# A bilinear form on one core: the first weights as two 64-partition halves, and smaller pieces at the end

**Chip, cores, metric.** One core of a Trainium2 chip. The metric is device time in microseconds (us), of the whole execution; the span that the profile shows is about 1.75 us shorter. In the profiles PE is TensorE, PEld its weight loads, DVE VectorE, ACT ScalarE, POOL GpSimd and SP SyncE; "clock" is the share of TensorE's full clock that was granted.

## The reference

```python
batch, dim_i, dim_j, dim_k = 32, 256, 256, 128        # all float32
np.einsum('bi,bj,kij->bk', x, y, weight)
```

The weights are 128 x 256 x 256 float32, 33.6 MB; x and y are 32 KB each.

## The kernel before

The outputs are done in 32 groups of 4 values of k. A group's weights are a tile of 128 partitions (32 pieces of i times 4 of k) by 8 x 256. Group 0 comes as float32 through SyncE's queue and is cast by ScalarE; groups 1 to 31 come through GpSimd's queue, cast to bfloat16 by the DMA, each into a buffer of its own.

```python
x_sb = consts.tile([B, I], f32);  nc.scalar.dma_start(out=x_sb, in_=x)
y_sb = consts.tile([B, J], f32);  nc.scalar.dma_start(out=y_sb, in_=y)
w0 = consts.tile([P, IC * J], f32)
nc.sync.dma_start(out=w0, in_=w_v[0])
def split(g):
    return [(0, 4), (4, 6), (6, 8)] if g == G - 1 else [(0, IC)]
# load(g): one GpSimd DMA for each piece of split(g), into its own bf16 tile
... # x_rep, transposes, mask products -> xblk; y -> y4; w0 cast to w0b
for g in range(G):
    ps = pso.tile([P, J], f32)
    for ic in range(IC):
        nc.tensor.matmul(out=ps, lhsT=xblk[:, ic], rhs=w_tiles[g, ic], ...)   # cut
    nc.vector.tensor_tensor_reduce(out=tmp, in0=ps, in1=y4, ..., accum_out=acc[:, g:g+1])
nc.sync.dma_start(out=out_v, in_=acc)
```

## Time and profile before

| | before |
|---|---|
| time, median | 88.63 us at first (3 runs), 88.59 beside the change (4 runs) |
| span of the profile (of a run of 88.90 us) | 87.1 us |
| busy: PE, DVE, POOL | 62%, 21%, 21% |
| DMA strip at 90% or more | 37 of 40 slices |
| last weights landed / PE done | 83.40 / 84.30 us |

The prediction below shows the lines that carry this. Two views are added here for comparison with those after. The first is the table of stretches for the head (columns: stretch, its length, busy time and count of PE, PEld, DVE, ACT and POOL, granted clock, DMA share, GB/s written):

```profile
3.00:4.00 1.00, 0.96 (x8) 0.94 (x8) 1.00 (x7) 0.00 (x0) 1.00 (x3) 1.00 0.89 318
4.00:5.00 1.00, 0.11 (x1) 0.00 (x0) 0.89 (x3) 0.00 (x0) 1.00 (x3) 1.00 0.92 353
5.00:6.00 1.00, 0.42 (x2) 0.28 (x2) 1.00 (x3) 0.00 (x0) 1.00 (x3) 1.00 1.15 320
```

While w0 flows as float32, 318 to 353 GB/s are written. The second is the page's list of DMA issues (KB each, us from issue to landing):

```profile
w<-in_weight_dram SPq DMA_DIRECT2D x1, 1024.0 KB, 5.3
...
x_sb<-in_x_dram ACTq DMA_DIRECT2D x1, 32.0 KB, 1.7
y_sb<-in_y_dram ACTq DMA_DIRECT2D x1, 32.0 KB, 4.0
```

x is there 1.7 us after its issue, w0 after 5.3.

### The profile page before, as it was taken

Reading aid. Unit: us, or ns where it says so; the run is one execution under the profiler, and the core shown is the slowest. Engines: PE = TensorE matmul, PEld = TensorE weight load, DVE = VectorE, ACT = ScalarE, POOL = GpSimd, SP = SyncE. Lnnn points to the kernel's source line nnn. Section 1 sums busy time; section 2 is a strip of 40 time slices with the busy share of each in tenths; the row PEclk is TensorE's granted clock in tenths of the full one; section 3 lists DMA queues with packets and bytes.
Section 4 is the critical chain, followed back from the end, with each engine's and each line's share of the span. In section 5 each row is a group of like instructions: output and inputs, shape, how many; then the busy total and the mean of one; then the engine's idle time right before and its main releaser. Section 6 shows DMA issues by size and latency. Waiting matters only on the chain.

```text
span 87.1 us, 741 instructions
## 1 busy us (share of the span) xinstructions
PE 54.4 (62%) x268; PEld 32.6 (37%) x268; DVE 18.6 (21%) x79; ACT 3.3 (4%) x3; POOL 18.3 (21%) x39
## 2 busy tenths in 40 slices
PE   0416994667777843776487773754887544974870
PEld 0415653433343432433344432332444331543630
DVE  0893123011111120111101111111011211031030
ACT  2327000000000000000000000000000000000000
POOL 5980222222111221112222222012222200000000
PEclk9999999755555696557955598589555975569659
DMA  1899999999999999999999999999999999999700
GB/s 30 277 312 209 216 216 216 213 213 213 213 214 213 211 213 218 213 216 213 213 213 213 211 216 213 211 213 216 213 218 211 213 214 211 214 214 203 127 3 8
DMA packets 5139, 17.43 MB, mean 200 GB/s; under 512 B 720, under 2 KB 1040, under 8 KB 5008
## 3 DMA queue, kind: packets, MB, share of 16 engines
q0 software_dynamic: 4752, 16.26, 93.6%
q1 hardware_dynamic: 288, 1.07, 3.5%
q10 hardware_dynamic: 96, 0.07, 0.4%
q8 instruction: 2, 0.03, 0.1%
q14 instruction: 1, 0.01, 0.0%
HBM read 33.62 MB, written 0.02 MB: 386 GB/s over the span
## 4 chain that ended last, share of the span: by engine, by line
DMA 87%; PE 4%; POOL 3%; issue 2%; DVE 0%; POOLq 0%; DVEq 0%
DMA w<-in_weight_dram 87%; PE ps L137 4%; POOL w L60 3%; DVE tmp L144 0%; POOL ident L68 0%; POOL ident L67 0%; POOLq L68 0%; POOLq L165 0%; DVEq L176 0%
## 5 line engine op out<-in xcount | busy, mean ns | idle before, releaser
L137 PE MATMUL ps<-w,xblk 128*128 128x256 bf16 x248 | 50.8, 377 | 24.2 <-DMA w<-in_weight_dram 24.2
L137 PEld LDWEIGHTS <-xblk 128*128 128x128 bf16 x256 | 31.0, 130 | 46.9 <-DMA w<-in_weight_dram 34.3
L60 POOL DMA_DIRECT2D w<-in_weight_dram x33 | 17.7, 546 | 50.6 <-DMA w<-in_weight_dram 49.8
L144 DVE CUSTOM_DVE_ANT_0 tmp<-ps,y 128x256 f32<-128x256 f32 x32 | 13.6, 425 | 62.2 <-PE ps L137 62.2
L137 PE MATMUL ps<-w0b,xblk 128*128 128x256 bf16 x8 | 2.1, 411 | 1.6 <-ACT w0b L129 1.6
L91 PE MATMUL xt_ps<-ident,x_rep 32*128 32x32 f32 x8 | 1.1, 293 | 3.0 <-POOL ident L68 3.0
L144 DVE DVE_READ_ACCUMULATOR2_ANT acc<- 128x1 f32 x32 | 2.7, 83 | 0.0
L100 DVE TENSOR_SCALAR xblk<-xt_ps,mask 128x256 bf16<-128x256 f32 x4 | 2.5, 771 | 0.1
L129 ACT CAST w0b<-w 128x1024 bf16<-128x1024 f32 x2 | 2.0, 1042 | 3.2 <-DMA w<-in_weight_dram 3.2
L91 PEld LDWEIGHTS xt_ps<-ident,x_rep 32*128 32x128 f32 x8 | 0.9, 200 | 3.0 <-POOL ident L68 3.0
L85 DVE COPY x_rep<-x_sb 32x128 f32<-32x128 f32 x8 | 1.3, 236 | 2.4 <-DMA x_sb<-in_x_dram 2.4
L129 ACT ACT_TABLE_LOAD x1 | 1.3, 1283 | 1.6 <-PEq L165 1.6
L109 PE MATMUL yt_ps<-ident,y_sb 32*128 32x32 f32 x2 | 0.4, 300 | 1.1 <-DMA y_sb<-in_y_dram 1.1
L109 PEld LDWEIGHTS yt_ps<-ident,y_sb 32*128 32x128 f32 x2 | 0.3, 199 | 1.2 <-DMA y_sb<-in_y_dram 1.2
L125 DVE COPY y<-y_ps 128x256 f32<-128x256 f32 x1 | 0.4, 425 | 1.3 <-PE y_ps L119 1.3
L119 PE MATMUL y_ps<-ident,yt 128*128 128x128 f32 x2 | 0.6, 417 | 0.0
L119 PEld LDWEIGHTS y_ps<-ident,yt 128*128 128x128 f32 x2 | 0.4, 226 | 0.1
L114 DVE COPY yt<-yt_ps 128x256 f32<-128x256 f32 x1 | 0.4, 448 | 0.0
L76 DVE TENSOR_REDUCE mask<-ident 128x4 f32<-128x128 f32 x1 | 0.4, 369 | 0.0
L68 POOL TENSOR_SCALAR_AFFINE_SELECT ident<-ident 128x128 f32<-128x128 f32 x1 | 0.3, 322 | 0.1
L67 POOL MEMSET ident<- 128x128 f32 x1 | 0.2, 224 | 0.0
L165 POOL MEMSET const-float32-0.0<- 128x1 f32 x1 | 0.1, 99 | 0.2 <-issue 0.2
(3 smaller groups left out, 0.3 us busy)
## 6 DMA issues: line engine op xcount, KB each, us to landing
w<-in_weight_dram POOLq DMA_DIRECT2D x30, 512.0 KB, 19.4
w<-in_weight_dram SPq DMA_DIRECT2D x1, 1024.0 KB, 5.3
w<-in_weight_dram POOLq DMA_DIRECT2D x1, 256.0 KB, 18.3
w<-in_weight_dram POOLq DMA_DIRECT2D x2, 128.0 KB, 15.6
x_sb<-in_x_dram ACTq DMA_DIRECT2D x1, 32.0 KB, 1.7
y_sb<-in_y_dram ACTq DMA_DIRECT2D x1, 32.0 KB, 4.0
out_dram<-acc SPq DMA_DIRECT2D x1, 16.0 KB, 1.4
```

The costliest lines, as they stand in the source:

```text
L60: nc.gpsimd.dma_start(out=wt, in_=w_v[g][:, :, lo * J:hi * J])
L76: nc.vector.tensor_reduce(out=mask, in_=ident.rearrange("p (ip kk) -> p kk ip", kk=KK), axis=mybir.AxisListType.X, op=add,)
L85: nc.vector.tensor_copy(out=x_rep[:, ic, :, :], in_=x_cols[:, ic, :].unsqueeze(2).to_broadcast([B, IP, KK]),)
L91: nc.tensor.transpose(out=xt_ps[:, ic, :], in_=x_rep[:, ic, :, :].rearrange("b ip kk -> b (ip kk)"), identity=ident[:B, :B],)
L100: nc.vector.tensor_scalar(out=xblk[:, :, :, kk], in0=xt_ps, scalar1=mask[:, kk:kk + 1], scalar2=None, op0=mult,)
L109: nc.tensor.transpose(out=yt_ps[:, jh, :], in_=y_sb[:, jh * P:(jh + 1) * P], identity=ident[:B, :B],)
L114: nc.vector.tensor_copy(out=yt4, in_=yt_ps.unsqueeze(3).to_broadcast([P, JH, B, KK]))
L119: nc.tensor.transpose(out=y4_ps[:, jh * P:(jh + 1) * P], in_=yt4[:, jh, :, :].rearrange("p b kk -> p (b kk)"), identity=ident,)
L125: nc.vector.tensor_copy(out=y4, in_=y4_ps)
L129: nc.scalar.copy(out=w0b[:, lo * J:hi * J], in_=w0[:, lo * J:hi * J])
L137: nc.tensor.matmul(out=ps, lhsT=xblk[:, ic, :, :].rearrange("p b kk -> p (b kk)"), rhs=w_tiles[g, ic], start=(ic == 0), stop=(ic == IC - 1),)
L144: nc.vector.tensor_tensor_reduce(out=tmp, in0=ps, in1=y4, scale=1.0, scalar=0.0, op0=mult, op1=add, accum_out=acc[:, g:g + 1],)
```

## The change

The intent: get the first weights under way sooner by issuing them from two queues at once and letting x and y wait; and shorten the work that is left when the last weights have landed.

```diff
-    x_sb = consts.tile([B, I], f32)
-    nc.scalar.dma_start(out=x_sb, in_=x)
-    y_sb = consts.tile([B, J], f32)
-    nc.scalar.dma_start(out=y_sb, in_=y)
     w0 = consts.tile([P, IC * J], f32)
-    nc.sync.dma_start(out=w0, in_=w_v[0])
+    PH = P // 2
+    with tc.manual_schedule(engines={mybir.EngineType.SP, mybir.EngineType.Activation}):
+        for h, eng in enumerate((nc.sync, nc.scalar)):
+            eng.dma_start(out=w0[h * PH:(h + 1) * PH, :],
+                          in_=w_v[0][h * PH // KK:(h + 1) * PH // KK])
+        x_sb = consts.tile([B, I], f32)
+        nc.scalar.dma_start(out=x_sb, in_=x)
+        y_sb = consts.tile([B, J], f32)
+        nc.sync.dma_start(out=y_sb, in_=y)
     def split(g):
-        return [(0, 4), (4, 6), (6, 8)] if g == G - 1 else [(0, IC)]
+        if g == G - 1:
+            return [(0, 4), (4, 6), (6, 7), (7, 8)]
+        if g == G - 2:
+            return [(0, 4), (4, 8)]
+        return [(0, IC)]
```

Below, "head" is the part down to y, "tail" is the new split.

More of the change, by code (lines that the diff above doesn't have):

```diff
@@ L41 @@
     w_v = weight.rearrange("(kk g) (ip ic) j -> g ip kk (ic j)", kk=KK, ic=IC)
-    x_sb = consts.tile([B, I], f32)
-    nc.scalar.dma_start(out=x_sb, in_=x)
-    y_sb = consts.tile([B, J], f32)
-    nc.scalar.dma_start(out=y_sb, in_=y)
     w0 = consts.tile([P, IC * J], f32)
-    nc.sync.dma_start(out=w0, in_=w_v[0])
-    def split(g):
-        return [(0, 4), (4, 6), (6, 8)] if g == G - 1 else [(0, IC)]
+    PH = P // 2
+    with tc.manual_schedule(engines={mybir.EngineType.SP, mybir.EngineType.Activation}):
+        for h, eng in enumerate((nc.sync, nc.scalar)):
+            eng.dma_start(
+                out=w0[h * PH:(h + 1) * PH, :],
+                in_=w_v[0][h * PH // KK:(h + 1) * PH // KK],
+            )
+        x_sb = consts.tile([B, I], f32)
+        nc.scalar.dma_start(out=x_sb, in_=x)
+        y_sb = consts.tile([B, J], f32)
+        nc.sync.dma_start(out=y_sb, in_=y)
+    def split(g):
+        if g == G - 1:
[3 more added lines that the diff above has]
+        return [(0, IC)]
     w_tiles = {}
```

## The prediction

> **What bounds the kernel now.** I read the page first: the busy rows, the strip of 40 slices, the chain that ended last.
>
> ```profile
> PE 54.4 (62%) x268; PEld 32.6 (37%) x268; DVE 18.6 (21%) x79; ACT 3.3 (4%) x3; POOL 18.3 (21%) x39
> ...
> DMA  1899999999999999999999999999999999999700
> ...
> DMA 87%; PE 4%; POOL 3%; issue 2%; DVE 0%; POOLq 0%; DVEq 0%
> ```
>
> No compute engine is full, while the DMA engines are at 90% or more in 37 of the 40 slices (2.2 us each). 87% of the chain is one thing, weights arriving. HBM read is 33.62 MB; one group is 1 MiB of float32, written as 0.5 MiB of bfloat16. In the trace's record of single packets, one engine starts a 4096-byte packet every 305 ns and a new group every 2.457 us: 8 packets are 2.440, so a group boundary costs 17 ns. 1.049 MB in 2.457 us is 427 GB/s read. This middle, about 31 x 2.457 = 76 us, is the floor; the change doesn't touch it. Only the head (before the stream flows) and the tail (after it stops) can move. For the head I read the order in time:
>
> ```profile
> 0.74 0.37 ACTq L44 DMA_DIRECT2D x_sb<-in_x_dram  x1
> 0.74 0.62 SPq L50 DMA_DIRECT2D w<-in_weight_dram  x1
> 1.14 0.45 ACTq L46 DMA_DIRECT2D y_sb<-in_y_dram  x1
> 1.24 0.66 POOL L60 DMA_DIRECT2D w<-in_weight_dram  x1 [0.80 <-POOLq L165]
> ...
> 2.42 1.33 DVE L85 COPY x_rep<-x_sb 32x128 f32<-32x128 f32 x8 [2.42 <-DMA x_sb<-in_x_dram]
> ...
> 6.09 1.99 ACT L129 CAST w0b<-w 128x1024 bf16<-128x1024 f32 x2 [3.19 <-DMA w<-in_weight_dram]
> ...
> 7.19 0.58 PE L137 MATMUL ps<-w0b,xblk 128*128 128x256 bf16 x2 [1.58 <-ACT w0b L129]
> ```
>
> Issues start at 0.74. By the packet records x moves from 1.75, w0 from 2.15; w0's packets last till 5.1 to 5.75, engine by engine, and on each engine the first packet of POOL's queue starts 6 ns after w0's last. So POOL's stream of groups 1 to 31 is ready and waits for w0: whatever w0 gains or loses moves the whole stream. For the tail, the chain in order of time:
>
> ```profile
> 61.29 19.52 DMA w<-in_weight_dram
> 80.81 0.05 issue
> 80.85 3.44 PE ps L137 x16
> 84.30 0.02 issue
> 84.32 0.42 DVE tmp L144
> ```
>
> The last 3.44 us are not a transfer. Group 30 lands whole at 80.81; then 16 matmuls run without a gap. By the semaphore records the pieces of group 31 land at 82.06, 82.76 and 83.40, while PE begins their matmuls at about 82.57, 83.42 and 83.85 (80.85 plus 8, 12, 14 steps of 0.214 us; 3.44 less the 0.417 duration of the last, over 15, is 0.20 to 0.21). PE is about 0.4 us behind the last landing. The granted clock there is halved:
>
> ```profile
> 81.50:82.00 0.50, 0.50 (x5) 0.36 (x3) 0.00 (x0) 0.00 (x0) 0.00 (x0) 0.50 0.86 139
> 82.00:82.50 0.50, 0.50 (x4) 0.38 (x3) 0.00 (x0) 0.00 (x0) 0.00 (x0) 0.50 0.22 35
> ```
>
> (Stretch, length, busy time of PE and PEld, then the other engines, clock, DMA share, GB/s.) PE is full at clock 0.50, while the DMA engines are already emptying. They empty unevenly: thirteen end by about 82.3, the last at 83.07. [...]
>
> [...] The trace of before[...]: w0's 1.049 MB from 2.15 to about 5.4 is some 320 GB/s. It has no 64-partition load of size, so it shows nothing on the halves. [...]
>
> **The change part by part.** (1) w0 as two 0.5 MB halves, issued at 0.74 on both queues. A transfer of 32 rows took 1.01 us from issue to first packet (0.74 to 1.75); w0, 1.41, behind x's. With a half on each queue and nothing ahead I put the first weight packet at 1.75 to 1.9: 0.25 to 0.4 us earlier. (2) x now moves inside the stream instead of in front of it: 32 packets of 45 ns over 16 engines plus two 9 ns completions, 0.1 us back. Head gain before contention: 0.15 to 0.3, say 0.25. (3) Contention on partitions: [...] My estimate is a median loss of 0.2, with a long tail.
>
> (4) x and y come later, behind halves: y took 4.0 us to land before, and now x will too, about 4.8 to 5.4 instead of 2.39. Behind it lie the copies (1.33), the transposes (about 0.3 more), four mask products (4 x 0.771, 2.5 with overlap): xblk at about 9.5 instead of 6.63, the first main matmul there instead of 7.19. That is 2.3 us late on PE, but not in the end: a group needs 8 x 0.214 = 1.7 us of PE against 2.457 us of arrival, so PE regains 0.7 per group and is level after four groups or so. Each group's weights have a buffer of their own, so POOL's issues wait for landings, never for PE.
>
> (5) Group 30 in two, group 31 ending in two single steps: two more issues on POOL at 0.53 us, done near 70 us, off the path. In the stream: two boundaries of 17 ns, plus the smaller packets. A 1024-byte packet costs 78.6 ns a start against 305 / 4 = 76.3, so about 3 ns is fixed per packet; 8 more packets of 2048 instead of 4096 cost 24 ns, 8 more of 512 another 24. In all 0.08 us later for the last landing, 83.48.
>
> (6) The tail with it: the first half of group 30 lands 1.23 us before the second, at 79.6, when PE is idle (group 29 ends at 79.5), so its four matmuls move into the gap. The second half at 80.85 ends by 81.5. Then PE waits for the first piece of 31, at 82.1: four to 82.98, two to 83.41, one to 83.62, and the last starts at 83.62, its weights there since 83.48, and ends 0.42 later, 84.04. Before: 84.28. Gain 0.24. The last split itself gives perhaps 0.05 of that; the split of group 30 does the rest.
>
> Sum: -0.25 head, +0.2 contention, -0.24 tail: -0.29 us. From 88.63: about 88.35, which I put as 88.4.
>
> **Rivals.** A: [...] w0 lands [...] later and drags the stream[...]. For it: [...] that POOL's stream waits for w0. Against: w0's first packets took 714 ns where later ones took 309[...]. Partly true is likely, wholly 1 in 8. B: the late x becomes the bound, PE never catches up. For: PE 62% busy at a mean clock of 0.73. Against: 24.2 us of idle time of PE behind weights, ten times the delay. It would cost at most 2.3 us if no slack were there; I give it under 3%. C: everything works, the halves overlap each other's start latency (0.4 us from 714 against 309), and the stragglers are milder: 0.4 more, 87.8. D: the tail isn't PE's but the last engine's: then the split gives nothing and costs 0.08; total near 88.6.
>
> **Range and chances.** Every part is small against 1.77 us, which 2% is. Upward only rival A reaches 89.5 or more[...]. Downward, head and tail at their best give 0.4 + 0.4, 87.8. So 87.8 to 89.5, with 4% for slower and 2% for faster.
>
> **What would show it.** The first weight packets near 1.8 instead of 2.15, and POOL's first group landing up to 0.3 earlier than 8.60: step 1; if it lands later, contention (step 3) is larger. The first CAST from w0 would move from 6.09 likewise. The first main matmul near 9.5 with PE level with the landings by group 6: step 4. In the chain, the run of 16 matmuls at the end replaced by one of about 8, behind a landing near 82: step 6. A final stretch where each matmul waits for its own landing would mean that DMA, not PE, sets the end. The middle, 2.457 us a group, must not change. Wrong would be: w0 landing after 7 us, a gap in the DMA strip between w0 and group 1, or PE still behind at 70 us.

The sum came to -0.29 us (-0.25 + 0.2 - 0.24). Its +0.2 (step 3) was worked out from no measured number; the other two terms are reckoned from the trace of before. Of the engine that ends last the trace shows two instruction fetches of 16 KB (0.94 and 0.98 us) and one of 8 KB (0.32 us), but not on which engine. That POOL's issues wait for landings and not for PE (step 4) is in before's list of waits: 25 times, 49.8 us, for weights by DMA, and once, 0.8 us, for POOL's own sequencer at the start.

## The result, and the profile after

Ratios are the mean time of one kernel's runs over that of the other's of the same rounds, so not quite the ratio of the medians quoted. Executions over 1.5% slower than the fastest of the same kernel are left out of the means.

| | before | after |
|---|---|---|
| time, median (4 runs each) | 88.59 us (88.46 to 88.67) | 89.77 us (89.54 to 89.95) |
| ratio, 95% interval | | 1.0132 (1.0103 to 1.0162) |
| span of the profile (runs of 88.90 and 89.54 us) | 87.1 | 87.8 |
| busy: PE, POOL | 62%, 21% | 59%, 22% |

The time went up by 1.2 us. It lies outside the range that the prediction gave, 87.8 to 89.5, on the slow side. First the head, the instructions in order of time after (start us, us, engine, line, operation):

```profile
0.74 0.66 SPq L49 DMA_DIRECT2D w<-in_weight_dram  x1
0.75 0.62 ACTq L49 DMA_DIRECT2D w<-in_weight_dram  x1
...
1.40 0.60 ACTq L54 DMA_DIRECT2D x_sb<-in_x_dram  x1
1.47 0.81 SPq L56 DMA_DIRECT2D y_sb<-in_y_dram  x1
...
8.40 1.16 DVE L95 COPY x_rep<-x_sb 32x128 f32<-32x128 f32 x8 [8.40 <-DMA x_sb<-in_x_dram]
...
12.52 0.61 PE L147 MATMUL ps<-w0b,xblk 128*128 128x256 bf16 x2 [2.38 <-DVE xblk L110]
```

Both halves are issued within 10 ns of each other. But x is there only at 8.40, and PE's first main matmul begins at 12.52 where it began at 7.19. The page's DMA issues after say how long the halves took:

```profile
w<-in_weight_dram SPq DMA_DIRECT2D x1, 512.0 KB, 6.7
w<-in_weight_dram ACTq DMA_DIRECT2D x1, 512.0 KB, 4.4
...
x_sb<-in_x_dram ACTq DMA_DIRECT2D x1, 32.0 KB, 7.0
```

The two halves, issued together, land 4.4 and 6.7 us later: one after the other, and the second later than the whole of w0 did (5.3). The same three stretches after show the rate:

```profile
3.00:4.00 1.00, 0.00 (x0) 0.00 (x0) 0.00 (x0) 0.00 (x0) 1.00 (x3) 1.00 1.21 262
4.00:5.00 1.00, 0.00 (x0) 0.00 (x0) 0.00 (x0) 0.00 (x0) 1.00 (x3) 1.00 0.97 262
5.00:6.00 1.00, 0.00 (x0) 0.00 (x0) 0.00 (x0) 0.00 (x0) 1.00 (x3) 1.00 0.84 180
```

The engines are as busy as before, but 262 and then 180 GB/s are written instead of 320 to 353. They are not starved; each packet takes longer. The trace's record of single packets has the start, duration, size and queue of each; the engine isn't in it and has to be worked out from which packet follows on which. By it, after the change an engine does its four packets of ScalarE's half, then its four of SyncE's, and only then POOL's. Before, a settled 8192-byte packet took 309 ns; after, the settled ones take 606 ns, and 44 of the second half's 64 are over 550.

Now the tail: the chain that ended last, its end in order of time (start us, us, what), after:

```profile
75.42 9.21 DMA w<-in_weight_dram
84.63 0.04 issue
84.67 0.28 PE ps L147
84.95 0.02 issue
84.98 0.42 DVE tmp L154
```

The run of 16 matmuls is gone. One matmul stands behind the last landing, 0.32 us from landing (84.63) to the end of PE (84.95); before it was 0.90 (83.40 to 84.30). But the two ends ran at different clocks, 0.50 before and 1.00 after, so the 0.58 us between them isn't the split's alone (see the tail's runs below). The landing itself is 1.23 later, and this takes back more than the tail can have given.

### The profile page after: what moved, and what is told of

It is laid out like the page before. It is cut to its first block, busy times and chain, and to the rows that moved or that the text cites. A ratio compares the mean times of both kernels' runs of the same rounds, so it can differ in the third digit from the quotient of the medians.

```text
span 87.8 us, 746 instructions
## 1 busy us (share of the span) xinstructions
PE 51.4 (59%) x268; PEld 31.3 (36%) x268; DVE 18.5 (21%) x79; ACT 3.3 (4%) x3; POOL 19.3 (22%) x41
## 4 chain that ended last, share of the span: by engine, by line
DMA 89%; issue 5%; POOL 1%; DVE 0%; PE 0%; POOLq 0%; DVEq 0%
DMA w<-in_weight_dram 89%; POOL w L70 1%; DVE tmp L154 0%; PE ps L147 0%; POOL ident L77 0%; POOLq L186 0%; POOLq L175 0%; DVEq L186 0%
## 5 line engine op out<-in xcount | busy, mean ns | idle before, releaser
L147 PE MATMUL ps<-w,xblk 128*128 128x256 bf16 x248 | 47.9, 359 | 22.4 <-DMA w<-in_weight_dram 22.3
L147 PEld LDWEIGHTS <-xblk 128*128 128x128 bf16 x256 | 29.7, 125 | 44.2 <-DMA w<-in_weight_dram 31.9
L70 POOL DMA_DIRECT2D w<-in_weight_dram x35 | 18.7, 545 | 56.3 <-DMA w<-in_weight_dram 55.5
```

What stands on the lines that cost most here:

```text
L70: nc.gpsimd.dma_start(out=wt, in_=w_v[g][:, :, lo * J:hi * J])
L147: nc.tensor.matmul(out=ps, lhsT=xblk[:, ic, :, :].rearrange("p b kk -> p (b kk)"), rhs=w_tiles[g, ic], start=(ic == 0), stop=(ic == IC - 1),)
```

## The experiments

To compare heads without the noise of the end I use two numbers from the packet records: **w0 per engine**, the summed durations of w0's packets over 16 engines, and **sixth transfer**, the mean over engines of the time at which POOL's sixth transfer (group 6) is done on it. A mean over engines is moved little by one late engine. Times of different rows come from different chips and rounds; the ratio is to the kernel before of the same rounds. The figures that stand first in the expectations of e1, e3 to e7, e10, e11 and e14 are those of the partition theory, the prediction's rival A: a half of w0 is slow because of which 64 partitions it covers. No run shows a mechanism.

| kernel | time, median us | ratio to before | w0 per engine us | sixth transfer us | last landing us |
|---|---|---|---|---|---|
| before | 88.59 | | 2.90 | 20.31 | 83.40 |
| after | 89.77 | 1.0132 | 4.04 | 21.27 | 84.63 |
| e16, after again | 89.68 | 1.0151 | 4.47 | 21.67 | 85.00 |
| e1, head only | 89.63 | 1.0138 | 3.98 | 21.21 | 84.54 |
| e2, e12, e15, tail only | 88.11, 87.90, 88.22 | 0.9984, 0.9962, 0.9970 | 2.60, 2.70, 3.06 | 19.93, 19.84, 20.13 | 83.10, 83.00, 83.40 |
| e8, group 30 in two only | 88.07 | 0.9970 | 2.73 | 19.84 | 83.11 |
| e3, w0 whole, x and y behind | 88.54 | 1.0029 | 2.55 | 20.18 | |
| e4, halves by columns, two queues | 89.32 | 1.0124 | 3.25 | 20.80 | |
| e9, halves by columns, one queue | 89.32 | 1.0114 | 3.68 | 21.07 | |
| e5, halves by partitions, one queue | 89.15 | 1.0090 | 3.48 | 20.67 | |
| e14, middle and outer partitions | 89.48 | 1.0086 | 2.90 | 20.55 | |

### Which part costs: head or tail

e1 has the new head with the old split; e2 the old head with the new split.

> The new head (w0 as two halves of 64 partitions on two queues, then x and y) with the old tail. [...] the halves[...] cost about 1.05 us at the first group of POOL's queue (landing 8.60 before, 9.65 after) and nothing gives it back, while the old tail has 0.4 us of PE lag: 89.6 to 90.1 us, slower than the whole change; most 8192-byte packets near 606 ns. Rival (the smaller pieces at the end are what costs): near 88.6, with packets near 309 ns.

> The old head with the new tail (group 30 in two, group 31 ending in two single steps). My sum: last landing 0.08 us later, PE no longer behind it, 0.25 to 0.45 us faster than before: 88.15 to 88.4. Rival (more pieces cost more in the stream than they give): 88.6 or above.

e1: 1.0138 (1.0076 to 1.0199), e2: 0.9984 (0.9936 to 1.0032). The whole loss is the head's. e1's packets show 606 ns again. e2 gained less than the 0.25 to 0.45 us expected. Its chain ends so:

```profile
73.36 9.74 DMA w<-in_weight_dram
83.10 0.04 issue
83.14 0.28 PE ps L141
83.42 0.02 issue
```

One matmul behind the last landing, 0.32 us. The old tail, in e1, ends so:

```profile
69.95 14.58 DMA w<-in_weight_dram
84.54 0.04 issue
84.58 0.39 PE ps L142 x2
84.97 0.02 issue
```

Two matmuls and 0.43 us, not 16 and 0.90 as in the trace of before. The kept traces tell the two apart by the clock. Twelve have the old tail: in six (e1, e3, e7, e9, e11, e13) the clock is back at 1.00 before PE is done, and PE ends 0.43 to 0.44 us after the last landing; in five (before, e4, e5, e10, e14) it is 0.50 to the end, and the lag is 0.90 to 1.11; e6 lies between. At full clock the new tail's 0.32 is thus only 0.11 us better. All six traces with group 30 cut end at clock 1.00. Whether the cut brings that about or it is chance isn't shown. How much that is worth in time one run couldn't say, so it was run twice more, once beside a kernel that only cuts group 30:

```diff
+        if g == G - 2:
+            return [(0, 4), (4, 8)]
         return [(0, 4), (4, 6), (6, 8)] if g == G - 1 else [(0, IC)]
```

> The old head with the new tail once more, for the size of the tail's gain (first time 0.9984, -0.5 to +0.3%). My sum said -0.24 us; the trace of the first time has the last landing to the end of PE 0.32 us where before has 0.90, and 0.08 us more stream, so -0.2 to -0.5 us. Rival (the end is set by the slowest DMA engine, PE's lag matters not): 0 to +0.1.

> The old head and only group 30 cut in two. My step 6 has this doing most of the tail's gain: 0.05 us or so less than the whole new tail, so -0.15 to -0.45 us from before. Rival (the single steps at the end do it): no gain, 0 to +0.1.

> The old head with the new tail a third time. If step 6 is right in size: ratio 0.996 to 0.998, as the first two (0.9984, 0.9962). Rival (no gain, the two were chance): 0.999 to 1.001.

0.9962 (0.9915 to 1.0008) and 0.9970 (0.9917 to 1.0023) for the tail; 0.9970 (0.9928 to 1.0011) for the cut of group 30 alone. No single interval excludes zero. The mean of the three tail runs is 0.9972, some 0.25 us; the direction is the same in all three and in e8, and the size is near 0.24. It sits in the slower runs: of the 33 runs of the kernel before beside these three, 15 took over 88.4 us, of the tail's 18 one, while the fastest are 87.88 and 87.77. It would fit if the cut spares the runs that end at half clock, but the kept traces can't show that; e8's own trace has 0.44 us of lag at clock 1.00, no less than the old tail there. e8 gives nearly all of it beside e12 in the same rounds, as step 6 said, but the difference between the two (0.0008) is far below what these runs can tell.

### Is it the order (x and y behind the weights)?

```diff
+        nc.sync.dma_start(out=w0, in_=w_v[0])
+        nc.sync.dma_start(out=x_sb, in_=x)
+        nc.sync.dma_start(out=y_sb, in_=y)
```

> w0 in one piece of 128 partitions on SyncE, first; x and y on the same queue after it; old tail. [...] w0's packets at 309 ns, x and y late without harm, 88.5 to 88.9. Rival (the order costs: x and y land late, PE starts late): 89.3 or more. It also shows whether w0's first packet comes earlier than 2.15 when nothing is ahead of it (my step 1 said 1.75 to 1.9; the profile after says 2.15 for a half, so size and not the place behind x would set it).

1.0029 (0.9979 to 1.0078), 88.54: hardly anything, though PE's first main matmul comes at 11.12 there. Late x and y do no harm that these runs can tell. And with nothing ahead of it on any queue, w0's first packet comes at 2.42, not earlier than before (2.15); in e10 and e11, where a whole w0 is also first, it comes at 2.15. So it isn't x that holds it back.

### Is it the partitions, or having two transfers?

> The head of the change, but w0 is cut by columns and not by partitions: two transfers of 128 partitions and 4096-byte rows on the same two queues at the same time, then x and y as in the change; old tail. [...] packets near 155 ns (half of 309), first POOL group landing near 8.6 to 8.8, 88.5 to 88.9. Rival (two queues at once, whatever the cut, cost): as slow as the head alone, 89.6 or more.

The diff to the change: `w0[:, h * CH:(h + 1) * CH]` from `w_v[0][:, :, h * CH:(h + 1) * CH]` in place of the partition halves. This was a miss for the partition theory: 1.0124, 89.32 us, nearly the 89.6 that the rival wanted. The packets say something more mixed: the second half ran mostly at 159 ns per 4096 bytes (mean 167), full speed, while in the change the second half ran at 606 per 8192; but the first half averaged 240 where 155 is half of 309. Two more kernels cut w0 on SyncE's queue alone:

> The kernel with w0 whole, then x and y, all on SyncE (88.54 us), with w0 cut in two halves of 64 partitions one after the other on that same queue. [...] packets near 606 ns all through, w0's time per engine 4.0 to 4.9 us instead of 2.55, 89.7 to 90.9 us. Rival (two queues beginning at once is what costs): 88.3 to 88.9, packets near 309 ns.

> The same, with w0 cut by columns into two transfers of 128 partitions and 4096-byte rows on one queue. If it is two queues at once that made the column halves slow (89.32 us): 88.3 to 88.9 here, packets near 157 ns. If it is the 4096-byte rows: 89.1 to 89.6 again, with the early packets at 200 ns and more. [...]

e5 (partition halves, one queue): 1.0090 (1.0026 to 1.0155), less than the partition theory wanted and more than the rival did. Its trace shows another order: on one queue an engine does half 0, then about five packets of POOL's, then half 1 packet by packet between POOL's. The second half's packets average 388 ns there, against 544 in the change, where none of POOL's run between them; that this makes the difference isn't shown. Half 0, which nothing else disturbed, slows down as in the change: its last 16 packets average 597 ns. e9 (column halves, one queue): 1.0114 (1.0054 to 1.0174), slow again. So two queues are not what makes column halves slow. That left rows of 4096 bytes, or the cut as such. Two kernels for that:

```diff
+        nc.sync.dma_start(out=w0, in_=w_v[0][:, :, 0:CH])     # e13: left columns only
+    nc.gpsimd.dma_start(out=w0r, in_=w_v[0][:, :, CH:])      # right columns by POOL, bf16
```

> w0's left columns alone (128 partitions, rows of 4096 bytes, one transfer on SyncE, then x and y); the right columns come by POOL as bfloat16 ahead of group 1. If rows of 4096 bytes are slow at the start by themselves (packets of 200 ns and more, as in both kernels with column halves): the same here, and no gain over w0 whole on SyncE, 88.5 or more. If it is the second transfer queued behind it that slows them: packets near 157 ns, and 88.0 to 88.6.

```diff
+        nc.sync.dma_start(out=w0[32:96, :], in_=w_v[0][8:24])      # e14
+        nc.scalar.dma_start(out=w0[0:32, :], in_=w_v[0][0:8])
+        nc.scalar.dma_start(out=w0[96:128, :], in_=w_v[0][24:32])
```

> w0 in parts of whole rows again, on two queues, [...] partitions 32 to 95 on SyncE, 0 to 31 and 96 to 127 on ScalarE, x and y behind on SyncE. [...] packets of 309 to 330 ns, none near 606, and w0's time averaged over engines 2.6 to 3.0 us against 4.0 in the change. Rival (cutting w0 into transfers begun together costs by itself, whichever partitions): 3.3 us and more. The time is no test: [...] 89 to 91 us.

e13: a single transfer with rows of 4096 bytes, nothing cut behind it on its kind of queue, averages 238 ns a packet, as the first halves of e4 did (240); 1.0037 (0.9973 to 1.0100) in time. So these early rows of 4096 bytes are slow by themselves, and e4 and e9 say little about the partitions. Why they are slow I don't know; rows of 4096 in e4's second half were not, nor were the first 16 packets of e13 and e4 (171 and 176 ns).

e14: w0 cut, two queues, whole rows, but no part that is just partitions 0 to 63 or 64 to 127. The outer 64 packets average 322 ns, none over 550. The middle 64 average 402, of which the first 16 carry the slow start (433 to 684, as in the kernel before: 487 to 745); the other 48 average 329, where the 48 of e5's half 0 (partitions 0 to 63, likewise first on SyncE) average 455. w0 per engine is 2.90, in the range of the uncut heads (2.55 to 3.06) and far from the change (3.98 to 4.47). Its time, 1.0086, is no test, as said: the spread of the engines at the sixth transfer is 19.38 to 21.55. Its mean of 20.55 is still some 0.5 above the uncut heads' 20.0; I can't assign all of that.

### Which partitions: the same load, shifted by 32

The cleanest test of the partitions adds a load that nobody reads, the same source rows once into partitions 0 to 63 and once into 32 to 95.

```diff
+    spare = consts.tile([P, IC * J], f32)
+    nc.sync.dma_start(out=spare[0:64, :], in_=w_v[0][0:P // 2 // KK])     # e6; e7: spare[32:96, :]
```

> The kernel before, with one extra load of 64 rows of 8192 bytes (0.5 MB, read by nobody) into partitions 0 to 63, behind w0 on SyncE. [...] four packets of 606 ns an engine, 2.4 us, minus what overlaps: 1.8 to 2.5 us over before, 90.1 to 90.9. Rival (a 64-partition load as such runs at full rate): 1.24 us, 89.4 to 89.8.

> The same extra load with the same source rows, into partitions 32 to 95 of the spare tile. [...] packets of 309 ns, 1.24 us over before, 89.4 to 89.8, about 1.2 us less than the load into partitions 0 to 63. If it is the number of partitions and not which ones: the same time as that load.

And the same on ScalarE's queue, beside w0 whole on SyncE:

> The kernel with w0 whole on SyncE, then x and y there (88.54 us), plus an extra 0.5 MB load of 64 rows into partitions 0 to 63 of a spare tile, issued on ScalarE at the same time, so that it goes ahead of POOL's stream like a half of the change. [...] its packets near 606 ns[...], the stream 1.9 to 2.4 us later than with w0 alone: 90.3 to 91.0. Rival (which partitions is indifferent; cutting is what costs): the same time as into partitions 32 to 95.

> The same extra load, same source rows, same queue, into partitions 32 to 95. [...] packets near 309 to 322 ns, 1.2 to 1.4 us later than with w0 alone, 89.7 to 90.1, and 0.6 to 1.1 us less than into partitions 0 to 63. Rival: equal to it within 0.2.

| extra load into | time us, ratio | its packets, mean ns | sixth transfer us |
|---|---|---|---|
| e6: 0 to 63, SyncE | 89.86, 1.0183 | 398 | 21.73 |
| e7: 32 to 95, SyncE | 89.57, 1.0155 | 323 | 21.36 |
| e10: 0 to 63, ScalarE | 90.05, 1.0201 | 436 | 21.86 |
| e11: 32 to 95, ScalarE | 89.75, 1.0156 | 330 | 21.44 |

Both pairs go the same way by the packets: 75 and 106 ns more a packet, four an engine, 0.30 and 0.42 us, and the stream is 0.37 and 0.42 us later. The two lists of DMA issues, of e10 and then of e11, show it as landings:

```profile
spare<-in_weight_dram ACTq DMA_DIRECT2D x1, 512.0 KB, 8.2
```

```profile
spare<-in_weight_dram ACTq DMA_DIRECT2D x1, 512.0 KB, 7.5
```

Nothing differs but the partitions written. e7 and e11 came out in their ranges, e6 and e10 below theirs (90.1 and 90.3 at least). The effect is smaller than expected (606 ns and over 0.6 us), and the extra load was not alone: by the packet records POOL's packets ran between its packets from 5.8 us on (in before, one of these writes 4096 bytes in 324 ns, one of w0's 8192 in 309). That this is the reason isn't shown. In the change nothing of POOL's runs until an engine has finished both halves (the first at 5.92 us). The times agree in direction, but their intervals overlap (1.0141 to 1.0261 against 1.0097 to 1.0216); the packets carry this, not the times. (In the profiled runs e10 ends at clock 0.50 and e11 at 1.00; such ends move single times too.)

### The change once more

> The whole change again beside it on the same chip. Head +1.1 to +1.3 us and tail -0.2 to -0.3 add up: 0.9 to 1.1 us over before, ratio 1.010 to 1.013, and the packets of the second half at 606 ns again. If the first measurement was partly chance (it had four runs): under 1.008.

1.0151 (1.0101 to 1.0201) beside e15's 0.9970. In its second half 48 of 64 packets are over 550 ns. 1.0151 is a little beyond the expected 1.010 to 1.013. Head and tail add up roughly: 1.0138 x 0.9972 is 1.011, against 1.0132 and 1.0151, within the intervals.

**The better version.** The tail alone, with the old head, is the fastest kernel here (87.90 to 88.22 against 88.19 to 88.41 for the kernel before beside it). It beats both, the change clearly and the kernel before by some 0.3%, which is at the edge of what these runs can show.

## Why the prediction was wrong, point by point

- **Step 1, head gain 0.25 us: wrong, it is zero.** The step was "With a half on each queue and nothing ahead I put the first weight packet at 1.75 to 1.9". The first weight packet came at 2.16 (before 2.15; e1 2.15, e16 2.14), and in e3 a whole w0 with nothing ahead at 2.42 (e10 and e11: 2.15). I had taken the wait between issue and first packet as a place in a line behind x. With nothing ahead it was no shorter: about 1.4 us for a half as for the whole (1.7 in e3), while x needed 1.0.
- **Step 2, x in the stream, 0.1 us:** not measured on its own. e3 with x and y both behind gives 1.0029, which fits and doesn't exclude zero.
- **Step 3, contention, "a median loss of 0.2": this is the step that failed.** I had assumed, from no trace, that parts of both halves would be written at the same time. Mostly they weren't. Every engine finished ScalarE's half first: partitions 64 to 127 were written from 2.16 to 4.49 us, 0 to 63 from 3.77 to 6.65. w0 per engine averages 4.17 us over the three kernels with the new head (4.04, 4.47, 3.98) and 2.80 over five with the old one (2.90, 2.60, 2.70, 3.06, 2.73): 1.37 us more. The sixth transfer is 1.37 us later too (21.38 against 20.01). e14, cut at other partitions, has 2.90; so by the packets' durations the cut has about 0.1 of the 1.37, and the rest goes with which partitions a part covers. By the sixth transfer e14 is some 0.5 late, so up to that much of the 1.37 may come with cutting; this stays open. One of the prediction's own signs of being wrong came true: SyncE's half landed at about 7.4 us (0.74 + 6.7), after 7.
- **Rival A** had this in kind (w0 lands later and drags the stream), and I gave it 1 in 8. Measured: the later half of w0 landed at 7.4 us where the whole had landed at 6.0 (0.74 + 5.3), and the stream came 1.37 later. In the packets one sees that the first of a half go well under 606 ns (the second 16: 326 to 350) and that before's first packets are slow as well. Rival C (the halves overlap each other's start) is out: no first packet came before 2.14 (and 88.35 less its 0.4 would be 87.95; 87.8 leaves the contention out as well).
- **Step 4, PE late but level after four groups:** right in kind, but the delay was put too small. I said first matmul at 9.5, and it was 12.52, because x waited for two slow halves and then moved between POOL's packets (landed by 8.4, not 5.4). It still cost nothing that the runs can tell (e3). The order of time of PE after:

```profile
14.63 6.09 PE L147 MATMUL ps<-w,xblk 128*128 128x256 bf16 x40
21.95 1.05 PE L147 MATMUL ps<-w,xblk 128*128 128x256 bf16 x8 [1.23 <-DMA w<-in_weight_dram]
```

  40 matmuls, groups 1 to 5, without a pause, at 0.152 us each and so faster than the 0.214 that I reckoned with; from group 6 on PE waits for weights again. Rival B (PE never catches up) is out.
- **Step 5, 0.08 us for more packets:** too small to be seen. The last landing in the tail kernels is 83.00 to 83.40, in before 83.40; the stream's own scatter covers it.
- **Step 6, -0.24 us from the tail:** right in direction and, as far as three runs can tell, in size (0.9972, some -0.25), but the size is partly luck. I counted the last matmuls at half clock and expected a run of about 8 at the end; the chain has one. In the trace after, the end ran at full clock:

```profile
82.00:83.00 1.00, 0.60 (x4) 0.29 (x3) 0.29 (x1) 0.00 (x0) 0.00 (x0) 1.00 1.14 163
83.00:84.00 1.00, 0.68 (x5) 0.47 (x6) 0.14 (x2) 0.00 (x0) 0.00 (x0) 1.00 0.25 35
```

  (Clock is the third number from the end.) PE busy 0.60 and 0.68 of each us, clock 1.00: it waits for each landing, where before it was full at 0.50. At full clock the old tail lags only 0.43, so there the split is worth 0.11; at half clock no trace shows the new one.
- **Rival D** (the last DMA engine sets the end, so the split gives nothing) is half true: after the change DMA does set the end, and so it does in the six traces of the old tail that end at full clock; in the trace of before PE's lag was real.
- **The sum.** Predicted -0.25 + 0.2 - 0.24 = -0.29. By the packet records and the tail's runs it is 0 + 1.37 - 0.25 = +1.1; measured +1.18 and, in e16, +1.43 by the medians.

The lesson of method: the trace of before already showed that POOL's stream began 6 ns after w0's last packet on every engine. There an engine finished one queue's transfer before it took the next. I read it as "POOL waits for w0" and didn't ask whether the two halves would run one after the other too. It was a hint and no rule: in the same trace y's packets ran between w0's from 3.29 us on, and in e5 and e10 the engines alternate between SyncE's or ScalarE's packets and POOL's. What decides it, no run here shows.

What stays open: why the rows of 4096 bytes of the first transfer are slow (e4, e9, e13); the 0.4 us or so by which e14's stream is late beyond its own packets; why a part that is just partitions 0 to 63 or 64 to 127 is written more slowly; whether the last single steps add anything to the cut of group 30; and whether that cut keeps the clock up at the end.

## What to carry to other kernels

Before cutting a transfer into halves for two queues, look in the trace at how the engines switch between queues, and at which partitions each part covers: the parts may run one after the other, as here, where a settled 8192-byte packet took 606 ns instead of 309 and all that was queued behind came 1.37 us later. If a load must be cut: here a part that covers partitions 32 to 95 had packets of 330 ns (e11), one that covers 0 to 63 packets of 436 (e10). And in this kernel, which streams for some 76 us, a late start of the compute engine did no harm that the runs can tell (e3: first main matmul at 11.12 instead of 7.19 us, time 1.0029), while giving the last groups smaller pieces took some 0.25 us off. Before comparing two ends of a kernel, look at the clock granted in each: 0.43 and 0.90 us of lag belong to the same tail here.
